# Later places on VectorE for the second half's delta rule, its convolution and pooling, and the last eight modulation sums

## The chip, the cores and the metric

The kernel runs on one core of a Trainium2 chip. The metric is the device time of one execution in microseconds; the figure for the kernel before is the median of three runs. One further execution was recorded by the hardware profiler, and all rows below come from it. Engines are named as in the profile: PE is TensorE (matmul) and PEld its weight loads, DVE is VectorE, ACT is ScalarE, POOL is GpSimd, and SP is SyncE, which issues most of the DMAs (SPq is its queue).

## What is computed

One layer of a streaming encoder for two groups of frames that share weights: a prompt of 1024 frames and a sample of 64 frames, width 1024. Cut to what matters:

```
mod = silu(c) @ w_ada + b_ada            # 6 x 1024: shift1, scale1, gate1, shift2, scale2, gate2
h   = rms_norm(x, norm_mix) * (1 + scale1) + shift1
u   = h @ w_in                           # columns of four mixers
mix = concat[conformer_conv, gated_deltanet, multiscale_pool, stick_breaking]
x   = x + gate1 * (mix @ w_out)
h2  = rms_norm(x, norm_ffn) * (1 + scale2) + shift2
x   = x + gate2 * ((silu(h2 @ w_gate) * (h2 @ w_up)) @ w_down)     # inner width 2816
```

The convolution mixer has 31 taps per channel and a layer norm; the delta rule works in chunks of 64 frames with a triangular solve in each and a state that goes from chunk to chunk; pooling takes windows of 2 to 16 frames; stick-breaking attention goes back over blocks of 128 keys. Besides `x`, the new caches and states are returned.

## The kernel before, in words

Everything is feature-major: a tile holds 128 features by up to 576 frames. The frames are cut in two halves: `HA` is prompt frames 0 to 511, `HB` is prompt frames 512 to 1023 with the 64 sample frames behind them. All products are in float32 made from three matmuls of rounded parts (`hi*hi`, `lo*hi`, `hi*lo`). So each weight tile of 128 x 1024 is loaded by SP (`load_w`, L320), rounded by ACT into `whi` and its rest taken by DVE into `wlo` (L330); activations are split in the same way into `hi` and `lo`. There are two buffers each for raw, `whi` and `wlo`.

The body (L1173 to L1188) calls the stages in this order: `in_proj(HA)`, `norm1(HB)`, `mixers(HA)`, `in_proj(HB)`, a part of the modulation sums, `out_proj(HA)`, the last eight modulation sums, `mixers(HB)`, `ffn(HA)`, `out_proj(HB)`, `ffn(HB)`. This is the order of tracing, not of execution: a planner replays the program against a time model and gives each engine one fixed queue. An instruction that is ready goes first by priority; priority follows the order of tracing, and what stands inside `tc.high_priority()` goes ahead of the rest. On the chip each engine then runs its queue in order and waits at the head of it.

The stages that the change touches:

- `out_proj` (L1035) loads the eight mixed tiles back from DRAM (`mixt`), splits them, makes 8 output tiles of 24 matmuls (`pg`), adds each to `x` (`residual`, L1029, tile `xA` or `xs`), sums squares into `acc`, and at the end runs the second norm (`modulate`, L308): a matmul over partitions (`pn`), Ln and Exp on ACT, and for each of eight tiles `nrm` (DVE), `hi` (ACT) and `lo` (DVE) in `modulate_k` (L297). For `HB` the splits of the mixed tiles go to `mixs`, on borrowed buffers, among them the buffer `raw` of the sample's modulation sums and of the delta rule.
- `ada_step` (L245) makes one modulation sum for the prompt: a load of 512 KB (`wadt`, in one of the two buffers `g0` and `g1`, which the feed-forward uses for its split too) and one DVE reduction. 24 of the 32 are made before `out_proj(HA)`; the last eight, for `gate2`, are traced behind it at high priority. `ada_sample` (L253) makes the 32 sums for the sample (`wads`, one buffer `raw`) inside `ffn(HA)` from the ninth tile on.
- `delta` (L855) runs short convolutions of four taps (`dnf`, `dn_feats`), decays, and `dn_group`: small batched matmuls, a triangular solve that goes out by DRAM (`nld`), is done on POOL (`fsn`, `fst`) and comes back by DRAM (`xd`, `X`), then the chain over chunks, and a store into `mixB`. For `HB` there are two groups of four chunks and one for the sample.
- `conv` (L870) makes for two tiles 31 taps each on DVE (`cy`, 606 columns for `HB`), a layer norm over partitions and a SiLU. `pool` (L984) makes ten sums on DVE and a small matmul.
- `ffn` (L1061) goes over 22 tiles in 11 chunks of two: gate and up products, the split `g` (`tg`, L1088 to L1091), and `down` for the chunk. In `ffn(HA)`, `conv(HB)` is traced at chunk 1 and `pool(HB)` at chunk 3. From chunk 6 on the products rotate over all eight PSUM banks. The last `down` of `HA` is held back and traced at the start of `ffn(HB)`.

`tc.issue_after(ins)`, which the kernel uses already for the modulation loads (`behind`, L317), puts every instruction that the block traces on the engine of `ins` behind `ins` in that engine's queue. Instructions of the block on other engines get no such place.

Of the kernel before, what the change touches and what calls it, by code (L numbers as in the profile page):

```python
# [11 lines left out]
ALU = mybir.AluOpType  # L12
# [16 lines left out]
KT = 8  # L29
FT = 22  # L30
FCH = 2
SAMP_DN = 515
SAMP_CV = 542
SAMP_PL = 527
# [25 lines left out]
def hybrid_encoder_kernel(ctx: ExitStack, tc: tile.TileContext, io):  # L60
    nc = tc.nc
# [5 lines left out]
    HA, HB = Half(), Half()  # L67
# [25 lines left out]
    def ST(name):  # L93
        return st.tile([P, 576], F32, tag="st", name=name)
# [18 lines left out]
    def act_(out, in_, func, bias=0.0, scale=1.0):  # L113
        nc.scalar.activation(out, in_, func, bias=bias, scale=scale)  # L114
# [5 lines left out]
        nc.vector.tensor_copy(out=out, in_=in_)  # L120

    def tt(out, a, b, op):
        nc.vector.tensor_tensor(out=out, in0=a, in1=b, op=op)  # L123

    def stt(out, a, s, b, op0, op1):
        nc.vector.scalar_tensor_tensor(out, a, s, b, op0, op1)  # L126

    def ts(out, a, s1, s2, op0, op1=None):
        if op1 is None:
# [13 lines left out]
    def f(ap):  # L143
        return ap.bitcast(F32)
# [152 lines left out]
    def modulate_k(h, k, r, sc, shift0, in_place):  # L297
        t = h.xt[k] if in_place else ST("nrm")
        h.hi.append(act.tile([P, 576], F32R, tag=f"hi{k}", name=f"hi{k}"))
        h.lo.append(act.tile([P, 576], F32R, tag=f"lo{k}", name=f"lo{k}"))  # L300
        for s0, w, g in h.segs:
            c = slice(s0, s0 + w)
            sh = mod[:, shift0 + k, g:g + 1]
            stt(t[:, c], h.xt[k][:, c], sc[:, k, g:g + 1], r[:, c], ALU.mult, ALU.mult)
            act_(h.hi[k][:, c], t[:, c], ACTF.Identity, bias=sh)
            stt(h.lo[k][:, c], t[:, c], sh, f(h.hi[k][:, c]), ALU.add, ALU.subtract)

    def modulate(h, acc, sc, shift0, in_place=False):  # L308
        r = rstd_of(h, acc, in_place)
# [3 lines left out]


    w_last = [None]

    def behind():  # L317
        return tc.issue_after(w_last[0])
# [551 lines left out]
    def conv(h):  # L870
        wn = SAMP_CV + 64 if h.samp else 512
        ys = []
        for i in range(2):
            g, e, buf = TT("cvg"), TT("cve"), TT("cvb")
            u = ud["cv", h.name]
            nc.sync.dma_start(out=g[:, 0:h.n], in_=u[2 * i + 1])
            nc.sync.dma_start(out=buf[:, 30:542], in_=u[2 * i, :, 0:512])
            if h.samp:
                copy_v(buf[:, 0:30], cvcar[:, i])
                nc.sync.dma_start(out=buf[:, 542:572], in_=io["ccs"][:, i])  # L880
                nc.sync.dma_start(out=buf[:, 572:636], in_=u[2 * i, :, 512:576])
            else:
                nc.vector.memset(buf[:, 0:30], 0.0)
            sigmoid_chain(e[:, 0:h.n], g[:, 0:h.n])
            tt(buf[:, 30:542], buf[:, 30:542], e[:, 0:512], ALU.mult)
            if h.samp:
                tt(buf[:, 572:636], buf[:, 572:636], e[:, 512:576], ALU.mult)
                nc.sync.dma_start(out=io["cv_s"][:, i], in_=buf[:, 606:636])
                nc.sync.dma_start(out=io["cv_p"][:, i], in_=buf[:, 512:542])
            else:  # L890
                copy_v(cvcar[:, i], buf[:, 512:542])
            y = fp.tile([P, 636], F32, tag=f"cy{i}", name=f"cy{i}")
            ts(y[:, 0:wn], buf[:, 0:wn], V("cw", 31 * i), V("cb", i), ALU.mult, ALU.add)
            for j in range(1, 31):
                stt(y[:, 0:wn], buf[:, j:j + wn], V("cw", 31 * i + j), y[:, 0:wn], ALU.mult, ALU.add)
            ys.append(y)
        hn = (wn + 1) // 2
        for c0 in range(0, wn, hn):
            n = min(hn, wn - c0)
            pm = PC("pmu")  # L900
            for i in range(2):
                mm(pm[:, 0:n], C("ones"), ys[i][:, c0:c0 + n], i == 0, i == 1)
            for i in range(2):
                stt(ys[i][:, c0:c0 + n], pm[:, 0:n], -1.0 / 256, ys[i][:, c0:c0 + n], ALU.mult, ALU.add)
        r = TT("cvr")
        sq = []
        for i in range(2):
            s = TT("cvs")
            act_(s[:, 0:wn], ys[i][:, 0:wn], ACTF.Square)
            sq.append(s)  # L910
        for c0 in range(0, wn, hn):
            n = min(hn, wn - c0)
            pm = PC("pvar")
            for i in range(2):
                mm(pm[:, 0:n], C("ones"), sq[i][:, c0:c0 + n], i == 0, i == 1)
            act_(r[:, c0:c0 + n], pm[:, 0:n], ACTF.Ln, bias=epst, scale=1.0 / 256)
        act_(r[:, 0:wn], r[:, 0:wn], ACTF.Exp, scale=-0.5)
        for i in range(2):
            y = ys[i]
            e = TT("cvz")  # L920
            tt(y[:, 0:wn], y[:, 0:wn], r[:, 0:wn], ALU.mult)
            ts(y[:, 0:wn], y[:, 0:wn], V("lng", i), V("lnb", i), ALU.mult, ALU.add)
            sigmoid_chain(e[:, 0:wn], y[:, 0:wn])
            tt(e[:, 0:wn], y[:, 0:wn], e[:, 0:wn], ALU.mult)
            nc.sync.dma_start(out=mixd[h.name][i, :, 0:512], in_=e[:, 0:512])
            if h.samp:
                nc.sync.dma_start(out=mixd[h.name][i, :, 512:576], in_=e[:, 542:606])
# [133 lines left out]
    def ffn(h):  # L1061
        if h.samp and DEFER:
            HA.last_down()
        n_ = h.n

        def gate(t):
            silu = h.samp or t >= SILU_T
            a = ST("fa")
            for ps, c0, n in gemm_fm(h, io["wgate"][t], h.hi, h.lo, KALL):
                with tc.high_priority():  # L1070
                    if not silu:
                        copy_a(a[:, c0:c0 + n], ps[:, 0:n])
                    else:
                        act_(a[:, c0:c0 + n], ps[:, 0:n], ACTF.Silu)
            if not silu:
                with tc.high_priority():
                    e = ST("fe")
                    sigmoid_chain(e[:, 0:n_], a[:, 0:n_])
                    tt(a[:, 0:n_], a[:, 0:n_], e[:, 0:n_], ALU.mult)
            return a  # L1080

        def up(t, a):
            j = t % FCH
            for ps, c0, n in gemm_fm(h, io["wup"][t], h.hi, h.lo, KALL):
                with tc.high_priority():
                    tt(a[:, c0:c0 + n], a[:, c0:c0 + n], ps[:, 0:n], ALU.mult)
            with tc.high_priority():
                tg = gp.tile([P, 1152], F32R, tag=f"g{j}", name=f"g{j}")  # L1088
                th, tl = tg[:, 0:576], tg[:, 576:1152]
                copy_a(th[:, 0:n_], a[:, 0:n_])  # L1090
                tt(tl[:, 0:n_], a[:, 0:n_], f(th[:, 0:n_]), ALU.subtract)  # L1091
            return th, tl

        def down(c, g, ms=range(KT)):
            mw = 8 // FCH
            for m in ms:
                if m % mw == 0:
                    w = load_w(io["wdown"][c, m // mw], 1024)
                o = (m % mw) * FCH * 128
                for ps, c0, n in gemm_fm(h, None, [t[0] for t in g], [t[1] for t in g], list(range(FCH)), w, o):  # L1100
                    with tc.high_priority():
                        residual(h, m, 40, ps, c0, n)
                if c == FT // FCH - 1:
                    nc.sync.dma_start(out=h.y[:, m], in_=h.xt[m][:, 0:n_])

        t0_s = 8
        a = gate(0)
        for c in range(FT // FCH):
            if not h.samp and c == 1:
                conv(HB)  # L1110
            if not h.samp and c == 3:
                pool(HB)
            g = []
            wide[0] = h.samp or c >= WIDE
            for j in range(FCH):
                if h.name == "A" and t0_s <= c * FCH + j:
                    s = c * FCH + j - t0_s
                    ada_sample(32 * s // (FT - t0_s), 32 * (s + 1) // (FT - t0_s))
                g.append(up(c * FCH + j, a))
                t = c * FCH + j + 1  # L1120
                a = gate(t) if t < FT else None
            if c == FT // FCH - 1 and DEFER and not h.samp:
                split_m = KT - 4 * DEFER
                down(c, g, range(split_m))
                h.last_down = lambda: down(c, g, range(split_m, KT))
            else:
                down(c, g)
# [34 lines left out]
        gemm_out(h, "pl", 2, 12)  # L1162

    def mixers(h):
        delta(h)
        sb_attn(h)
        if h.samp:
            sb_sample()
        else:
            conv(h)  # L1170
            pool(h)
# [7 lines left out]
        ada_step()  # L1179
    scale2(0)  # L1180
    out_proj(HA)
    with tc.high_priority():
        while ada_left:
            ada_step()
    mixers(HB)
# [179 lines left out]
```

## Time and profile before

| | us |
|---|---|
| median of three runs (lowest, highest) | 1485.28 (1483.03, 1486.69) |
| the profiled execution | 1488.28 |
| its span | 1486.4 |
| mean granted clock of TensorE | 0.975 |
| PE busy | 1405.1 (95%) |
| DVE busy | 1028.0 (69%) |
| ACT busy | 661.5 (45%) |
| POOL busy | 125.4 (8%) |

Busy is the time in which an engine has an instruction at work; matmul ends are modelled, so a busy TensorE is not one at its peak. The granted clock is a share of 2.4 GHz; it has two levels, 1.00 and 0.50 (1.2 GHz), and a value between them is a mean over a stretch. Times in rows are counted from the start of the span. In a row of a timeline the columns are start, duration, engine, line of the kernel, operation, output<-inputs and shapes, the number of merged instructions, and in brackets how long the engine stood before it and what ended that. A line is often that of a helper (L126 is every `scalar_tensor_tensor`, L138 every plain matmul); the tile's name tells which step it is.

### The profile page before, as it was taken

What the parts mean: (1) busy time and instruction counts of PE and PEld (TensorE: products, weight loads), DVE (VectorE), ACT (ScalarE), POOL (GpSimd) and SP (SyncE); (2) the same over time, 40 slices, a digit from 0 to 9 for tenths busy, and PEclk for the clock granted to TensorE, in tenths of its full rate; (3) what the DMA queues carried; (4) which work ended last, traced back from release to release, by engine and by line L of the source; (5) the groups of instructions that cost most, each with busy time, mean ns of one, the idle gap of its engine ahead of it and who ended that gap; (6) DMA issues with size and microseconds to landing.
All of it is one profiled execution on the core that took longest, in us unless ns stands there. A gap on an engine that the chain in (4) does not pass through costs nothing.

```text
span 1486.4 us, 24762 instructions
## 1 busy us (share of the span) xinstructions
PE 1405.1 (95%) x9824; PEld 1223.4 (82%) x9824; DVE 1028.0 (69%) x1816; ACT 661.5 (45%) x1191; POOL 125.4 (8%) x246
## 2 busy tenths in 40 slices
PE   8999999979987699799999899999899999999998
PEld 5777888858965477587777688889799999999998
DVE  7888897964799899766867666664744555544444
ACT  4457644745564368656755422222522222222221
POOL 0003100410004000600230000000000000000000
PEclk9999999989998899899999999999999999999999
DMA  8675655574745323424544454542322222222222
GB/s 294 239 228 166 202 168 166 155 213 146 260 153 168 75 75 95 123 81 129 161 113 153 155 186 154 177 158 83 110 92 86 86 82 77 84 86 86 86 83 95
DMA packets 98547, 205.43 MB, mean 138 GB/s; under 512 B 30848, under 2 KB 40928, under 8 KB 98432
## 3 DMA queue, kind: packets, MB, share of 16 engines
q1 hardware_dynamic: 89888, 191.68, 39.7%
q0 software_dynamic: 8544, 12.17, 3.9%
q8 instruction: 77, 1.26, 0.4%
q14 instruction: 38, 0.31, 0.1%
HBM read 175.57 MB, written 28.24 MB: 137 GB/s over the span
## 4 chain that ended last, share of the span: by engine, by line
PE 63%; DVE 17%; DMA 11%; issue 4%; ACT 3%; POOL 2%; SPq 1%; DVEq 0%; ACTq 0%; POOLq 0%
PE pg L138 57%; DMA wadt<-in_wadat_dram 4%; DVE cy L126 3%; DVE wlo L123 3%; DVE lo L126 1%; PE psC L141 1%; DMA X<-xd 1%; DVE dnf L126 1%; DVE junk L212 1%; PE pw L138 1%; PE z L141 1%; DVE wadt L212 1%; DVE nrm L126 1%; DMA raw<-udnB 1%; POOL fst L135 1%
## 5 line engine op out<-in xcount | busy, mean ns | idle before, releaser
L138 PE MATMUL pg<-hi,whi 128*128 128x288 f32 (+1 forms) x1504 | 504.8, 337 | 13.4 <-ACT whi L117 3.7
L138 PE MATMUL pg<-hi,wlo 128*128 128x288 f32 (+1 forms) x1504 | 499.7, 333 | 1.6 <-DVE wlo L123 1.6
L138 PE MATMUL pg<-lo,whi 128*128 128x288 f32 (+1 forms) x1504 | 498.7, 332 | 2.0 <-DVE lo L126 2.0
L117 ACT ACTIVATE whi<-wraw 128x1024 fp32r<-128x1024 f32 (+2 forms) x192 | 199.7, 1041 | 489.1 <-PE pg L138 419.4
L138 PEld LDWEIGHTS pg<-hi,whi 128*128 128x128 f32 x1504 | 285.4, 190 | 45.2 <-issue 5.7
L123 DVE TENSOR_TENSOR wlo<-wraw,whi 128x1024 fp32r<-128x1024 f32 (+2 forms) x192 | 230.6, 1202 | 111.9 <-ACT whi L117 107.4
L138 PEld LDWEIGHTS pg<-lo,whi 128*128 128x128 f32 x1504 | 285.6, 190 | 27.2 <-DVE lo L126 3.0
L138 PEld LDWEIGHTS pg<-hi,wlo 128*128 128x128 f32 x1504 | 285.0, 190 | 27.3 <-DVE wlo L123 3.2
L138 PE MATMUL pg<-g,whi 128*128 128x288 f32 (+1 forms) x1056 | 253.5, 331 | 3.0 <-DVE xA L126 1.9
L138 PEld LDWEIGHTS pg<-g,whi 128*128 128x128 f32 x1056 | 178.2, 189 | 20.1 <-DVE xA L126 4.3
L138 PE MATMUL pg<-g,wlo 128*128 128x288 f32 (+1 forms) x528 | 172.0, 329 | 0.0
L126 DVE SCALAR_TENSOR_TENSOR xs<-pg,mod,xs 128x288 f32<-128x288 f32 (+2 forms) x288 | 106.5, 412 | 85.7 <-PE pg L138 84.0
L138 PEld LDWEIGHTS pg<-g,wlo 128*128 128x128 f32 x528 | 99.6, 189 | 7.5
L123 DVE TENSOR_TENSOR fa<-fa,pg 128x288 f32<-128x288 f32 (+1 forms) x66 | 35.0, 531 | 101.8 <-PE pg L138 98.7
L126 DVE SCALAR_TENSOR_TENSOR cy<-cvb,vec,cy 128x512 f32<-128x512 f32 (+1 forms) x120 | 94.0, 796 | 0.2
L126 DVE SCALAR_TENSOR_TENSOR xA<-pg,mod,xA 128x512 f32<-128x512 f32 x96 | 69.3, 745 | 17.0 <-PE pg L138 16.4
L212 DVE CUSTOM_DVE_ANT_0 wadt<-wadt,cb,vec 128x1024 f32<-128x1024 f32 x32 | 41.0, 1282 | 22.8 <-DMA wadt<-in_wadat_dram 22.6
L114 ACT ACTIVATE e<-e 128x512 f32<-128x512 f32 (+4 forms) x100 | 52.1, 521 | 0.9
L138 PE MATMUL pg<-mixs,whi 128*128 128x288 f32 x256 | 50.8, 295 | 0.0
L212 DVE CUSTOM_DVE_ANT_0 wads<-wads,cb,vec 128x1024 f32<-128x1024 f32 x32 | 41.1, 1283 | 11.6 <-DMA wads<-in_wadat_dram 11.2
L114 ACT ACTIVATE zs<-zs 128x512 f32<-128x512 f32 (+4 forms) x50 | 25.9, 517 | 38.5 <-DVE zs L123 36.5
L138 PEld LDWEIGHTS pg<-mixs,whi 128*128 128x128 f32 x256 | 41.0, 188 | 0.1
(299 smaller groups left out, 1857.0 us busy)
## 6 DMA issues: line engine op xcount, KB each, us to landing
wraw<-in_wgate_dram SPq DMA_DIRECT2D x44, 512.0 KB, 3.3
wraw<-in_wup_dram SPq DMA_DIRECT2D x44, 512.0 KB, 3.2
wraw<-in_wdown_dram SPq DMA_DIRECT2D x44, 512.0 KB, 3.3
wadt<-in_wadat_dram SPq DMA_DIRECT2D x32, 512.0 KB, 4.7
wads<-in_wadat_dram SPq DMA_DIRECT2D x32, 512.0 KB, 4.1
wraw<-in_wfm_dram SPq DMA_DIRECT2D x30, 512.0 KB, 3.6
wraw<-in_wout_dram SPq DMA_DIRECT2D x16, 512.0 KB, 3.4
xA<-in_xa_dram SPq DMA_DIRECT2D x16, 256.0 KB, 5.2
```

The lines of the kernel that those rows point to most:

```text
L114: nc.scalar.activation(out, in_, func, bias=bias, scale=scale)
L117: nc.scalar.activation(out, in_, ACTF.Copy)
L123: nc.vector.tensor_tensor(out=out, in0=a, in1=b, op=op)
L126: nc.vector.scalar_tensor_tensor(out, a, s, b, op0, op1)
L135: nc.gpsimd.tensor_tensor(out=out, in0=a, in1=b, op=op)
L138: return nc.tensor.matmul(out, lhsT=lhsT, rhs=rhs, start=start, stop=stop)
L141: nc.tensor.matmul(out, lhsT=lhsT, rhs=rhs, start=start, stop=stop, skip_group_check=True)
L212: nc.vector.tensor_tensor_reduce(out=junk, in0=w, in1=cbt[g], scale=1.0, scalar=V("b_ada", col), op0=ALU.mult, op1=ALU.add, accum_out=mod[ ...
```

## The change

Three blocks get a place on DVE by `issue_after`. `tt` and `stt` now return their instruction, and `v_last` holds the last such instruction of two sites: the `lo` of a norm's tile (`modulate_k`) and the rest `tl` of a feed-forward tile (`up`).

- The last eight modulation sums are put behind the last `lo` of the first half's second norm.
- `delta(HB)` is put behind the same instruction; `delta(HA)` is not changed.
- `conv(HB)` and `pool(HB)` are traced together at chunk 5 of `ffn(HA)` instead of chunks 1 and 3, behind the `tl` of tile 9, the last of the fifth chunk.

```diff
+CONV_C = 5
...
     def tt(out, a, b, op):
-        nc.vector.tensor_tensor(out=out, in0=a, in1=b, op=op)
+        return nc.vector.tensor_tensor(out=out, in0=a, in1=b, op=op)
...
     def stt(out, a, s, b, op0, op1):
-        nc.vector.scalar_tensor_tensor(out, a, s, b, op0, op1)
+        return nc.vector.scalar_tensor_tensor(out, a, s, b, op0, op1)
...
-            stt(h.lo[k][:, c], t[:, c], sh, f(h.hi[k][:, c]), ALU.add, ALU.subtract)
+            v_last[0] = stt(h.lo[k][:, c], t[:, c], sh, f(h.hi[k][:, c]), ALU.add, ALU.subtract).ins
...
     w_last = [None]
+    v_last = [None]
...
-                tt(tl[:, 0:n_], a[:, 0:n_], f(th[:, 0:n_]), ALU.subtract)
+                v_last[0] = tt(tl[:, 0:n_], a[:, 0:n_], f(th[:, 0:n_]), ALU.subtract).ins
...
         for c in range(FT // FCH):
-            if not h.samp and c == 1:
-                conv(HB)
-            if not h.samp and c == 3:
-                pool(HB)
+            if not h.samp and c == CONV_C:
+                with tc.issue_after(v_last[0]):
+                    conv(HB)
+                    pool(HB)
...
     def mixers(h):
-        delta(h)
+        if h.samp:
+            with tc.issue_after(v_last[0]):
+                delta(h)
+        else:
+            delta(h)
         sb_attn(h)
...
     out_proj(HA)
-    with tc.high_priority():
+    with tc.high_priority(), tc.issue_after(v_last[0]):
         while ada_left:
             ada_step()
     mixers(HB)
```

## Rows read from the trace of the kernel before

**Rows 1.** The page, first part: busy us, share, instructions of each engine.
```profile
PE 1405.1 (95%) x9824; PEld 1223.4 (82%) x9824; DVE 1028.0 (69%) x1816; ACT 661.5 (45%) x1191; POOL 125.4 (8%) x246
```

**Rows 2.** Stretches: busy us (instructions) of each engine, granted clock, DMA share, GB/s.
```profile
407.00:410.00 3.00, 0.72 (x5) 0.41 (x3) 2.14 (x5) 1.15 (x3) 0.00 (x0) 1.00 0.56 201
410.00:527.00 117.00, 91.82 (x682) 68.45 (x683) 109.47 (x173) 59.46 (x106) 22.80 (x44) 0.88 0.44 125
527.00:620.00 93.00, 88.33 (x595) 68.09 (x593) 91.54 (x164) 74.33 (x148) 26.46 (x44) 0.98 0.37 111
...
775.00:984.00 209.00, 205.12 (x960) 164.23 (x959) 140.43 (x202) 74.39 (x112) 0.75 (x1) 0.99 0.51 166
840.00:976.00 136.00, 135.48 (x582) 110.54 (x582) 86.64 (x116) 40.83 (x51) 0.00 (x0) 0.99 0.54 175
1050.00:1075.00 25.00, 20.61 (x118) 17.87 (x116) 18.59 (x39) 14.40 (x26) 0.00 (x0) 0.93 0.26 86
```

**Rows 3.** DVE groups, 410 to 527 us: count | busy, mean ns | idle before.
```profile
L126 DVE SCALAR_TENSOR_TENSOR cy<-cvb,vec,cy 128x606 f32<-128x606 f32 x36 | 30.4, 851 | 0.0
...
L212 DVE CUSTOM_DVE_ANT_0 wadt<-wadt,cb,vec 128x1024 f32<-128x1024 f32 x8 | 10.1, 1276 | 4.5 <-DMA wadt<-in_wadat_dram 4.5
L126 DVE SCALAR_TENSOR_TENSOR dnf<-raw,vec,dnf 128x256 f32<-128x256 f32 x18 | 8.3, 486 | 0.0
...
L126 DVE SCALAR_TENSOR_TENSOR nrm<-xA,s,acc 128x512 f32<-128x512 f32 x8 | 5.6, 747 | 0.0
```

**Rows 4.** DVE timeline around the first half's second norm.
```profile
493.35 0.68 DVE L123 TENSOR_TENSOR acc<-acc,sq 128x512 f32<-128x512 f32 x1
...
500.45 1.28 DVE L212 CUSTOM_DVE_ANT_0 wadt<-wadt,cb,vec 128x1024 f32<-128x1024 f32 x1 [4.45 <-DMA wadt<-in_wadat_dram]
...
506.35 2.74 DVE L126 SCALAR_TENSOR_TENSOR nrm<-xA,s,acc 128x512 f32<-128x512 f32 x4
...
525.42 0.74 DVE L126 SCALAR_TENSOR_TENSOR lo<-nrm,mod,hi 128x512 fp32r<-128x512 f32 x1
```

**Rows 5.** ACT timeline there: the reciprocal root of the norm.
```profile
495.98 0.63 ACT L114 ACTIVATE acc<-acc 128x512 f32<-128x512 f32 x1
```

**Rows 6.** PE timeline at full clock: matmuls of 512 columns one after another.
```profile
414.85 0.39 PE L138 MATMUL pg<-hi,wlo 128*128 128x512 f32 x1
415.08 0.40 PE L138 MATMUL pg<-hi,whi 128*128 128x512 f32 x1
```

**Rows 7.** PE waits near 475, 620 and 760 us: us in total, times, longest.
```profile
PE pw L138 <- DMA X<-xd: 7.9, 1, 7.9
...
PE pw L138 <- DMA X<-xd: 6.3, 1, 6.3
...
PE pw L138 <- DMA X<-xd: 2.6, 1, 2.6
```

**Rows 8.** SP timeline: last stores of convolution, pooling and delta rule.
```profile
611.73 0.43 SPq L927 DMA_DIRECT2D mixB<-cvz  x1
...
684.38 0.43 SPq L1019 DMA_DIRECT2D mixB<-plm  x1
...
806.80 0.38 SPq L853 DMA_DIRECT2D mixB<-kbe  x1
```

**Rows 9.** DMA issues: count, KB each, us to landing.
```profile
wadt<-in_wadat_dram SPq DMA_DIRECT2D x32, 512.0 KB, 4.7
```

**Rows 10.** Instructions on the tile cy alone, 394 to 615 us: busy us, columns PE PEld DVE ACT.
```profile
394.00:615.00 221.00, 2.52 (x8) 1.44 (x8) 59.09 (x74) 2.61 (x4) 0.94 0.44 127
```

**Rows 11.** DVE timeline: first tap, a pooling sum, fifth chunk's last split, last sample sum.
```profile
396.31 0.59 DVE L132 TENSOR_SCALAR cy<-cvb,vec 128x606 f32<-128x606 f32 x1
...
602.15 0.78 DVE L123 TENSOR_TENSOR pls<-plb 128x605 f32<-128x605 f32 x1
...
775.14 0.68 DVE L123 TENSOR_TENSOR g<-fa,g 128x512 fp32r<-128x512 f32 x1
...
982.66 1.28 DVE L212 CUSTOM_DVE_ANT_0 wads<-wads,cb,vec 128x1024 f32<-128x1024 f32 x1 [0.44 <-DMA wads<-in_wadat_dram]
```

## The prediction

> **What bounds the kernel now.** The page's first part comes first: TensorE is busy 95% of the span, 1405.1 of 1486.4 us, and VectorE 69% [rows 1]. So a change that moves VectorE work can only win TensorE's waits and the time it runs at its lower clock. The stretches come next: they say where these are. In 840 to 976 us TensorE waits 0.5 us of 136 at clock 0.99, but from 410 to 527 us it is busy 91.8 of 117 us at a granted clock of 0.88, while VectorE is busy 109.5 of 117 [rows 2]. In that stretch stand the first half's output projection and its second norm. Third, the groups of VectorE there: 36 convolution taps of the second half take 30.4 us, the eight modulation sums 10.1 us, the delta rule's short convolution 8.3 us [rows 3]. None of these is what the norm waits for, yet they stand in its queue. The timeline shows it: the last partial sum of squares starts at 493.35 us, ScalarE has the reciprocal root at 496.6 (495.98 + 0.63), but the first `nrm` starts only at 506.35, because VectorE stood 4.45 us at a modulation sum whose weights had not landed, and then did another [rows 4, 5]. The last `lo` ends at 526.2.
>
> **What moves.** Three groups get a later place on VectorE. None gets a new semaphore: an instruction is only put behind another of the same engine; its followers on ScalarE, TensorE, GpSimd and SyncE's queue wait for its data as before.
>
> A. *Second norm freed.* Of the 109.5 us of VectorE in 410 to 527 the taps (30.4), the sums (10.1) and the delta rule (8.3 for its taps, and some twenty operations on 512 columns at the 0.68 us of such a row [rows 4]) leave, about 60 us in all. About 50 us stay. TensorE then sets the pace: one matmul of 512 columns starts each 0.227 us [rows 6], eight output tiles of 24 make 43.7 us, five attention blocks of eight such matmuls 9 us. The tail is a sum over partitions (1 us), Ln and Exp (1.3 us) and 16 operations of VectorE, four of which take 2.74 us together [rows 4], so 11 us. Thus 410 + 43.7 + 9 + 13 = 476 us for the last `lo`, 50 us earlier. But the 50 us are not the gain: the delta rule's matmuls that filled this stretch must still be done, so only TensorE's losses count. They are 3 - 0.72 = 2.3 us before 410, 25.2 us of waits after it, and the low clock: 0.88 over 117 us is 28 us at 1.2 GHz; part of it lies on the waits, 14 us I take as busy, half of it lost: 7. Together 34 us. New losses: without the delta rule the norm has little to cover it. The nearest row is the second half's own norm, 1050 to 1075 us, where the first half's held-back last down product (48 matmuls, 11 us) is the cover: 4.4 us of waits and clock 0.93 [rows 2], which is 6 us; without cover 6 + 11 = 17. Attention covers a little: I take 14. A = -34 + 14 = -20 us (bounds -28 and -17 by the two prices of the norm, and 0 if TensorE finds as little to do as before).
>
> The Trainium skill (Perfetto Trace Analysis, Optimization Strategy under Identifying Performance Opportunities) speaks against A: where the most-contended engine changes over time, it advises to interleave the regimes, and this change takes an interleaving apart. By that rule A would be about 0 and the sum +11 instead of -9. The rows so far go against it: the interleaved stretch 410 to 527 has the lowest clock and the most waits of those shown [rows 2]. It is a rival below.
>
> B. *Delta rule later.* Its three triangular solves go over GpSimd and DRAM, and each time TensorE, in order, stood at the result: 7.9, 6.3 and 2.6 us [rows 7]. The first lies inside A's losses; moved into the feed-forward it does not vanish, because feed-forward matmuls queued behind it stand as well. The nearest row is the second, which is already there: 6.3, and about 1 for the clock: B = +7 us (0 if the plan has enough ahead of it, +10 if it is the first one's 7.9 with its clock). SyncE's stores of the solve's input move along; a weight load queued behind one may come late: 0 to +3, I take 0, since two weight tiles are in flight. The delta rule's last store is at 806.8 us now [rows 8]. It starts at most some 90 us later than now, so it ends by 897; its output is needed near 984 us, so 87 us cover it, and what lies beyond would be paid in full.
>
> *Eight sums.* They cost 10.1 us behind the norm, beside the first feed-forward tiles. Two buffers and 4.7 us per load [rows 9] make three more rounds of 4.7 + 2 x 1.3, so they end near 476 + 22 = 498 us. Their buffers are those of the feed-forward's first split (needed by the first down product, some 27 us of matmuls after 476) and their values scale that product: covered by 5 us; uncovered at most 10.
>
> C. *Chunks 0 to 4 without the convolution.* In 527 to 620 VectorE is busy 91.5 of 93 us and TensorE loses 4.7 us of waits and 2 by the clock [rows 2]. The delta rule takes the convolution's place there, so little goes: -2 us (0 to -6).
>
> D. *Chunks 5 to 10 with convolution and pooling.* The convolution's operations are busy 59.1 us in 394 to 615 [rows 10], about 5 us more for its gates; neighbours overlap by 0.08 us (0.747 alone [rows 3], 2.74 for four), which leaves 57. Pooling has ten operations of about 0.78 us [rows 11]: 8. The fifth chunk's last split now starts at 775.1 us [rows 11]; from there to 984, where the last sample sum ends and the second half's projection gets its buffer, VectorE is busy 140.4 of 209 us [rows 2]. Add 65, and 10 for the delayed end of the delta rule: 215 us. VectorE reached 94% (109.5 of 117) and 98% (91.5 of 93) with such a mix; at 97% this takes 222 us. TensorE needs 209 and 7 for what comes with it, 216. D = 222 - 216 = +6 us (0 at full density, +12 at 94%). This is the term I trust least.
>
> **Sum.** -20 + 7 - 2 + 6 = -9 us. The profiled execution took 1488.28 us, 1.9 more than its span; that makes 1479.3. The median of the runs shown is 3.0 us lower, so 1476 for what is timed.
>
> **Rivals.**
>
> 1. *VectorE sets chunks 5 to 10 and takes the gain back.* If the fifth chunk ends only 12 us earlier and VectorE keeps 94% there, D is +12, and with B at +10 the sum is -20 + 10 - 2 + 12 = 0: 1485. For it: the 215 us against some 209. Against: conv taps are always ready, and filled VectorE to 98% in 527 to 620.
>
> 2. *The convolution comes late for the second half's projection: slower.* Now convolution and pooling go from 396.3 us (first tap) to 684.8 (last store), 288 us, the convolution alone to 612, 216 us [rows 8, 11]. From 760 us (775 less the 15 gained by A, B and C) they have until 975, 9 us before the projection's split less store and load. So it decides from 215 us on. At the convolution's own 216 us with 8 for store, load and split the end comes 9 us late: 1485; at the pace of both, 288, it is 73 late: 1549. The modulation sums for the sample columns stand in this queue too: the last starts at 982.66, just ahead of the split that needs its buffer [rows 11]; a delay there stops the projection as well. Against: the old pace was shared with a norm and the delta rule, the new one is not. As a typical price I take +20 over the forecast: 1496.
>
> 3. *More is won.* The first solve's stall finds cover (B = 0), the norm costs only 6 us (A = -28), and attention and delta rule, in a less crowded queue, save 6 us (C = -6), D = +6: -28: 1457.
>
> 4. *Un-interleaving costs what it saves* (A = 0): 7 - 2 + 6 = +11: 1496. For it: TensorE's other matmuls in 410 to 527 are gone. Against: 25 us of waits with them there.
>
> That the change does nothing is hardly possible: the taps stand in the norm's queue by name.
>
> **Chances.** Forecast 0.44 (its own range 1466 to 1481), rival 1 0.19 (1481 to 1490), rival 2 0.14, rival 3 0.16, rival 4 0.07. About 0.3%, 4.5 us, is what a measurement of this kernel can tell from no change. Faster: 0.42 of the forecast, all of rival 3 and a little of rival 1, 0.60. Slower: rivals 2 and 4 and a little of rival 1, 0.21. Within: 0.19. The range goes from 1455, which leaves half of rival 3's lower side out, to 1497, which leaves out rival 2's tail: 1455 to 1497.
>
> **What would show it.** A: no `cy`, `dnf` or `wadt` between the first `lo<-mixt` and the last `lo<-nrm`; that last `lo` near 476 us (before 490: right; after 505: wrong); waits and low clock there under 20 us. B: `pw` waiting for `X` three times, 15 us or more, now all in the feed-forward. Sums: no wait of `g` for `wadt`. C: TensorE waits in the first five chunks about as now. D: VectorE over 94% from the first convolution tap to the first split of `mixs`; the last `mixB<-cvz` before that split. The prediction is wrong if TensorE waits over 10 us ahead of the second half's projection for convolution, pooling or the sample sums, or if the last `lo` comes no earlier than 505 us.

## The result: 1.7% slower

The changed kernel takes 1509.64 us (median of four runs, 1508.08 to 1511.28), the kernel before on the same chip 1484.15: a ratio of 1.0173 [1.0149, 1.0198], 25 us slower. 1476 us were forecast, and 1455 to 1497 as the range. The profiled execution took 1509.31 us, its span 1507.4.

The first part of the page after, engine by engine, against [rows 1]: as many instructions on each engine, and TensorE busy 9.4 us longer, while the mean granted clock went from 0.975 to 0.962.

```profile
PE 1414.5 (94%) x9824; PEld 1227.7 (81%) x9824; DVE 1026.7 (68%) x1816; ACT 665.3 (44%) x1191; POOL 120.9 (8%) x246
```

Where the time went is read from stretches. First the changed kernel (columns as in [rows 2]: stretch, busy us and instructions of PE, PEld, DVE, ACT, POOL, granted clock, DMA share, GB/s):

```profile
250.00:380.00 130.00, 126.68 (x1219) 110.75 (x1218) 79.70 (x137) 71.36 (x149) 25.01 (x49) 0.99 0.65 205
410.00:527.00 117.00, 103.96 (x521) 79.95 (x520) 96.88 (x181) 75.04 (x138) 5.70 (x10) 0.93 0.41 119
527.00:620.00 93.00, 85.27 (x653) 68.06 (x652) 61.74 (x101) 57.73 (x108) 22.66 (x42) 0.94 0.34 88
711.00:1006.00 295.00, 258.80 (x1419) 200.18 (x1414) 225.02 (x347) 114.27 (x196) 23.23 (x46) 0.91 0.45 139
780.00:830.00 50.00, 38.11 (x206) 27.60 (x205) 49.59 (x86) 21.93 (x49) 9.15 (x14) 0.86 0.29 85
830.00:880.00 50.00, 32.14 (x179) 22.43 (x180) 25.66 (x48) 15.74 (x33) 10.83 (x28) 0.69 0.38 113
880.00:930.00 50.00, 46.73 (x201) 37.13 (x200) 32.47 (x43) 15.90 (x20) 0.00 (x0) 1.00 0.62 199
```

The kernel before, in the stretches of these that [rows 2] does not have:

```profile
250.00:380.00 130.00, 118.07 (x1122) 101.50 (x1121) 87.37 (x165) 75.89 (x166) 23.31 (x49) 0.93 0.55 168
...
780.00:830.00 50.00, 50.00 (x278) 38.73 (x278) 36.57 (x59) 27.55 (x50) 0.75 (x1) 1.00 0.48 156
830.00:880.00 50.00, 46.12 (x190) 36.37 (x189) 33.31 (x46) 17.75 (x25) 0.00 (x0) 0.97 0.53 169
880.00:930.00 50.00, 50.00 (x218) 40.84 (x218) 28.75 (x37) 13.25 (x16) 0.00 (x0) 1.00 0.49 163
```

I count as TensorE's loss in a stretch its idle time and the busy time times (1 - clock):

| stretch, us | before: idle + clock | after: idle + clock | after less before |
|---|---|---|---|
| 250 to 380 | 11.9 + 8.3 | 3.3 + 1.3 | -15.6 |
| 410 to 527 | 25.2 + 11.0 | 13.0 + 7.3 | -15.9 |
| 527 to 620 | 4.7 + 1.8 | 7.7 + 5.1 | +6.3 |
| 780 to 930 | 3.9 + 1.4 | 33.0 + 15.3 | +43.0 |

The sum is +17.8, and the span grew by 21.0 us. So 31.5 us are won in two stretches ahead of 527, and 43 are lost in 150 us. The stretches left out come to about +7 by the same measure, so it is some 4 us too high for the whole; it lies ahead of 250 us, where the profiles of all the kernels here differ by up to 11 us, that of e7 from the kernel before by 8. Chunks are counted from 0, as in the code: the fifth chunk is chunk 4, and `CONV_C = 5` is the one behind it. The next fence is VectorE's timeline after: the second norm's first `nrm`, its last `lo`, the fifth chunk's last split, the first tap and the last sample sum (against [rows 4, 11]).

```profile
449.53 0.74 DVE L127 SCALAR_TENSOR_TENSOR nrm<-xA,s,acc 128x512 f32<-128x512 f32 x1
...
461.21 1.41 DVE L127 SCALAR_TENSOR_TENSOR lo<-nrm,mod,hi 128x512 fp32r<-128x512 f32 x2
...
711.50 0.69 DVE L124 TENSOR_TENSOR g<-fa,g 128x512 fp32r<-128x512 f32 x1
...
717.21 0.60 DVE L133 TENSOR_SCALAR cy<-cvb,vec 128x606 f32<-128x606 f32 x1
...
1004.72 1.28 DVE L213 CUSTOM_DVE_ANT_0 wads<-wads,cb,vec 128x1024 f32<-128x1024 f32 x1 [1.49 <-DMA wads<-in_wadat_dram]
```

The norm is over at 462.6 us in place of 526.2, and the fifth chunk's split stands 63.6 us earlier. Much of that lead is mixers put off; what is left of it, and more, goes where they come due: the last sample sum, which frees the second half's projection, ends at 1006.0 us in place of 983.9. TensorE's waits after, 780 to 900 us (waiting matmul, what it waited for, us in total, times, longest):

```profile
PE pw L139 <- DMA X<-xd: 8.0, 1, 8.0
PE py L139 <- DVE W L124: 4.4, 2, 2.8
PE pg L139 <- DVE xA L127: 4.3, 1, 4.3
PE pg L139 <- DVE wlo L124: 4.0, 3, 1.6
PE psOs L142 <- ACT ph L118: 3.4, 1, 3.4
...
PE pvar L139 <- ACT cvs L115: 1.3, 1, 1.3
```

No wait is over 8.0 us. TensorE's timeline shows why they add up:

```profile
824.36 0.40 PE L139 MATMUL pg<-hi,wlo 128*128 128x512 f32 x1
...
831.19 0.42 PE L142 MATMUL psOs<-ph,v2s 128*128 128x64 f32 x1 [3.40 <-ACT ph L118]
...
834.29 2.37 PE L139 MATMUL pmu<-cy,cst 128*128 128x303 f32 x4
837.96 2.39 PE L139 MATMUL pvar<-cvs,cst 128*128 128x303 f32 x4 [1.31 <-ACT cvs L115]
848.32 0.45 PE L139 MATMUL pw<-cst,X 64*64 64x64 f32 x2 [7.97 <-DMA X<-xd]
...
854.39 0.69 PE L139 MATMUL py<-W,X 64*64 64x64 f32 x8 [1.63 <-DVE W L124]
854.87 0.64 PE L139 MATMUL px<-X,W 64*64 64x64 f32 x8
855.43 0.79 PE L139 MATMUL pg<-hi,whi 128*128 128x512 f32 x1
```

From 824.8 to 855.4 us its queue holds no feed-forward product (`pg`), only the sample attention (`psOs`, `psCs`), the convolution's layer norm (`pmu`, `pvar`) and the delta rule's sample group (`pw`, `py`, `px`), each waiting for the one before or for another engine. This is chunk 6, where the feed-forward begins to turn over all eight PSUM banks (`WIDE = 6`; `BANKS` is two of `mm`, two of `dn`, and `cv`, `z`, `c`, `o`). `dn` are the delta rule's, `cv` the convolution's, the last three the attention's. In the kernel before no mixer but the sample attention was left by then: convolution and delta rule had stored at 611.7 and 806.8 [rows 8].

Which bank the next product stood for can be read from the program. Each product takes the next entry of `BANKS`; the first of chunk 6, the up product of tile 12, is the program's 143rd and takes `o` (143 modulo 8 is 7), the bank of `psOs`. Gate and up product of tile 13, in `mm`, went ahead of it up to 824.8; the gate product of tile 14 has `dn`, and the downs need tile 12. The sample attention's last product ends near 834.5, but its four heads leave the bank one by one through a single buffer, `sbo`, and ScalarE twice waited until the head before was stored. The last of the four copies on VectorE ends at 854.6, and the product starts at 855.4:

```profile
845.01 0.22 ACT L118 ACTIVATE sbo<-psOs 64x64 f32<-64x64 f32 x1 [4.11 <-DMA mixB<-sbo]
...
854.36 0.22 DVE L124 TENSOR_TENSOR sbo<-psOs,sbo 64x64 f32<-64x64 f32 x1
```

### The profile page after: what moved, and what is told of

The parts are those of the page before. It is cut to its first block, busy times and chain, and to the rows that moved or that the text cites. A ratio compares the mean times of both kernels' runs of the same rounds, so it can differ in the third digit from the quotient of the medians.

```text
span 1507.4 us, 24783 instructions
## 1 busy us (share of the span) xinstructions
PE 1414.5 (94%) x9824; PEld 1227.7 (81%) x9824; DVE 1026.7 (68%) x1816; ACT 665.3 (44%) x1191; POOL 120.9 (8%) x246
## 4 chain that ended last, share of the span: by engine, by line
PE 69%; DVE 15%; DMA 7%; issue 3%; ACT 3%; POOL 1%; SPq 1%; DVEq 0%; ACTq 0%; POOLq 0%
PE pg L139 58%; DVE cy L127 2%; DVE wlo L124 2%; PE psC L142 2%; DMA wadt<-in_wadat_dram 2%; PE pk L139 2%; PE psO L142 1%; DVE xA L127 1%; ACT whi L118 1%; DMA wads<-in_wadat_dram 1%; DMA X<-xd 1%; PE z L142 1%; DMA mixt<-mixA 1%; DVE dnf L127 1%; DVE lo L127 1%
## 5 line engine op out<-in xcount | busy, mean ns | idle before, releaser
L115 ACT ACTIVATE fa<-pg 128x288 f32<-128x288 f32 (+1 forms) x52 | 22.3, 429 | 40.6 <-PE pg L139 40.5
```

## Experiments

Convolution here is always convolution with pooling. The expectations name three theories. **P**: from chunk 6 on the feed-forward needs banks that late mixers still hold, so its products can't be queued between them. **V**: VectorE, full of taps (49.59 of 50 us in 780 to 830), makes all behind it late. **Q**: the mixers' short chains cost the same wherever they stand. Each ratio is to the kernel before on the same chip.

| kernel | median us | ratio [95%] |
|---|---|---|
| e1 changed, two banks in all chunks | 1503.54 | 1.0164 [1.0137, 1.0191] |
| e2 changed, convolution behind chunk 1 | 1508.85 | 1.0197 [1.0165, 1.0229] |
| e3 convolution and pooling alone, chunk 5 | 1512.45 | 1.0225 [1.0195, 1.0255] |
| e4 delta rule and sums alone | 1497.51 | 1.0107 [1.0067, 1.0147] |
| e5 changed, WIDE 8 | 1496.91 | 1.0074 [1.0050, 1.0098] |
| e6 as e2, WIDE 8 | 1490.61 | 1.0052 [1.0033, 1.0071] |
| e7 before, WIDE 8 | 1492.35 | 1.0063 [1.0041, 1.0085] |
| e8 as e4, WIDE 8 | 1492.61 | 1.0064 [1.0040, 1.0087] |
| e9 convolution alone, chunk 1 | 1504.85 | 1.0140 [1.0097, 1.0183] |
| e10 convolution alone, chunk 3 | 1503.75 | 1.0137 [1.0091, 1.0184] |
| e11 as e3, WIDE 8 | 1491.96 | 1.0050 [1.0027, 1.0073] |
| e12 as e9, with the eight sums | 1510.26 | 1.0175 [1.0136, 1.0214] |
| f1 as e9, five banks in chunks 6 and 7 | 1488.63 | 1.0055 [1.0020, 1.0091] |
| f2 changed, same five banks | 1530.62 | 1.0338 [1.0295, 1.0381] |
| f3 before, same five banks | 1483.27 | 0.9997 [0.9978, 1.0015] |
| f4 as e9, WIDE 8 | 1494.90 | 1.0093 [1.0058, 1.0129] |
| g1 as f1, behind chunk 3 | 1477.36 | 0.9968 [0.9951, 0.9985] |
| g2 as f1, behind chunk 2 | 1473.34 | 0.9943 [0.9927, 0.9960] |

**The halves and the banks at all (e1 to e4).**

```
e1: -WIDE = 6      +WIDE = 11     # of 11 chunks: never
e2: -CONV_C = 5    +CONV_C = 1
e3: delta(h) and the eight sums without issue_after, as before
e4: conv(HB) at chunk 1 and pool(HB) at chunk 3 without issue_after, as before
```

> The changed kernel, with the first half's feed-forward kept to its own two PSUM banks in all eleven chunks (WIDE 11 in place of 6), so none of its products asks for a bank that the convolution's norm, the sample attention or the delta rule's sample group still holds. Theory P (banks): TensorE's loss between 780 and 905 us comes from products of chunks 6 and 7 that stand in order behind those banks; without them feed-forward products fill the gaps, and some 25 to 40 us return: 1470 to 1485 us. Theory V (VectorE is full, 99% in 730 to 830 us, and everything behind the convolution comes late): the banks are no cause, 1500 to 1512 us. Theory Q (the short products of the mixers stand in TensorE's queue one behind the other whatever the banks are): also 1500 to 1512.

> The changed kernel with convolution and pooling queued behind the first chunk's last split (CONV_C 1 in place of 5); the delta rule and the eight sums stay behind the second norm. Theory P: convolution and its norm are done near 700 us, ahead of chunk 6, and only the delta rule's sample group still holds a bank: 1475 to 1490 us, with the second norm still done near 462 us. Theory V: the crowding only moves into chunks 1 to 5, where taps and delta rule share VectorE: 1490 to 1505. If the delta rule's later place is the cause by itself: 1500 or more.

> The kernel before with only the convolution and pooling moved behind the fifth chunk; delta rule and eight sums where they were. Theory P: the convolution's norm and the sample attention come later than chunk 6's first product, which takes their banks: 1495 to 1515 us although nothing of the delta rule is late. If the delta rule's place is the cause: 1475 to 1490, since the second norm loses 30 us of taps ahead of it and nothing else is late.

> The changed kernel with convolution and pooling where they were before (chunks 1 and 3, no order edge); only the delta rule and the eight sums are behind the second norm. If the convolution's place is the cause of the loss: 1470 to 1485 us, with some of the gain at the norm gone since taps stand in its queue again. If the delta rule's place is the cause: 1495 or more, with TensorE's gaps at chunk 6 as in the changed kernel.

Each half alone is slower (e3, e4), so no one part is to blame, and the parts don't add: 33 and 16 us by the ratios against 25 together. An early convolution (e2) does not help: it came out above P's and V's numbers, where the delta rule's place by itself had been put. e1, which P put at 1470 to 1485, came out near the changed kernel. Its stretches show two things in one number:

```profile
830.00:880.00 50.00, 42.66 (x221) 32.11 (x220) 30.46 (x52) 24.52 (x36) 11.94 (x25) 0.91 0.38 116
...
930.00:980.00 50.00, 45.29 (x183) 34.54 (x182) 31.25 (x43) 11.65 (x14) 0.00 (x0) 0.97 0.50 176
```

The gap shrinks (busy 42.7 in place of 32.1, clock 0.91 in place of 0.69), but two banks lose 4.7 us in 930 to 980, where eight lose none. By idle and clock as above e1 loses 30 us in 780 to 930 where the changed kernel loses 48, and 22 in 930 to 1100 in place of 7. So the turn is worth having, only later. In e3 a product waits for a bank by name; here and below the columns are those of the waits, and this is 780 to 930 us of e3:

```profile
PE ppl L139 <- DVE plo L127: 7.7, 1, 7.7
PE pg L139 <- DVE xA L127: 7.3, 6, 2.7
PE pg L139 <- DVE sbo L124: 6.4, 1, 6.4
```

`sbo` is the copy that frees the sample attention's bank; a feed-forward product can wait for it only by that bank.

**The turn two chunks later (e5 to e8).** One line in each of four kernels:

```
-WIDE = 6
+WIDE = 8
```

> The changed kernel with the feed-forward's turn over all eight PSUM banks begun at chunk 8 (WIDE 8), when the mixers are done, in place of chunk 6. In the run with two banks throughout TensorE's gap at 830 to 880 us went from 17.9 to 7.3 us, but it then lost 4.7 us of 50 and more in 930 to 980, where chunks on eight banks lose nothing. Theory P (the turn over eight banks meets mixers that still hold theirs): both are had, 20 us less than 1503: 1480 to 1492 us. Theory V (VectorE full of taps in 730 to 830 is what makes the rest late): 1497 to 1510. Theory Q (the delta rule's solves and other short chains cost the same wherever feed-forward stands behind them): 1497 to 1510.

> As the run before this one, with convolution and pooling behind the first chunk (CONV_C 1, WIDE 8). Theory P with V (both the banks and the crowded VectorE have to go): 1470 to 1485 us. Theory P alone: as with CONV_C 5, 1480 to 1492. Theory Q: 1497 or more.

> The kernel before with WIDE 8 in place of 6, a control. Theory P: there the mixers are done when chunk 6 begins (last sample product at 825 us), so eight banks cost nothing in chunks 6 and 7 and two banks lose: 1490 to 1505 us, slower than before. If WIDE 8 is simply better, whatever the mixers do: below 1480, and the banks say nothing of the change.

> Delta rule and eight sums behind the second norm, convolution and pooling where they were, WIDE 8. Theory P: the 8.5 us stand at the sample group's solve at 840 to 848 us gets feed-forward products of two banks in front of it: 1472 to 1487 us. Theory Q: 1495 to 1500, as with WIDE 6.

The same line gains 1.0% on the changed kernel and 1.4% on e2, and costs the kernel before 0.6%. With WIDE 8 the change stands at 1.0074 / 1.0063 = 1.0011 (about [0.998, 1.004] from the two intervals) of its own before: of 25 us next to nothing is left, though no gain either. That is what shows P, as an interaction. But it returned less than P alone had promised: e5's 1496.9 lies above P's 1492, at the lower edge of what V and Q gave, and e8's 1492.6 lies between P's 1487 and Q's 1495. e5, 780 to 930 us, its stretches and waits:

```profile
780.00:830.00 50.00, 42.84 (x249) 31.60 (x249) 49.60 (x85) 25.21 (x54) 4.38 (x7) 0.93 0.38 116
830.00:880.00 50.00, 41.38 (x201) 30.73 (x200) 33.66 (x55) 23.03 (x33) 18.15 (x35) 0.90 0.36 110
880.00:930.00 50.00, 41.69 (x209) 31.36 (x208) 32.30 (x48) 21.15 (x32) 0.00 (x0) 0.93 0.61 186
```

```profile
PE pg L139 <- DVE xA L127: 12.8, 5, 5.5
PE pw L139 <- DMA X<-xd: 7.0, 1, 7.0
```

24.1 us are still idle there. 12.8 are products that wait for a bank whose result VectorE has not yet added (`xA`), behind taps; with the taps at chunk 1 (e6) that wait is 2.1 us, and 9.6 us are idle in all, as in the kernel before with the same line (e7). That is V's part; in the times it is 6 us, with intervals that overlap. The rows of e6 and e7:

```profile
780.00:930.00 150.00, 140.38 (x797) 108.86 (x794) 95.75 (x158) 73.58 (x128) 23.89 (x46) 0.98 0.49 146
...
780.00:930.00 150.00, 140.13 (x653) 108.01 (x652) 95.52 (x137) 57.00 (x88) 0.75 (x1) 1.00 0.48 152
```

**Convolution alone, and early (e9 to e12).**

```
e9, e10: as e3, with CONV_C = 1, 3;  e11: as e3, with WIDE = 8;  e12: as e9, and
-    with tc.high_priority():
+    with tc.high_priority(), tc.issue_after(v_last[0]):    # the eight sums
```

> The kernel before with only convolution and pooling moved, and only behind the first chunk's last split (CONV_C 1): the taps leave the second norm's queue, the delta rule stays early, and all mixers should be done before chunk 6 begins its turn over eight banks. Theory P: the gain at the norm stays (in the conv-only run with CONV_C 5 the lost time to 680 us was some 35 us less than before) and nothing is paid at chunk 6: 1460 to 1476 us. Theory Q or V (each gain there is paid later by the same work, wherever it stands): 1480 to 1495.

> The same behind the third chunk (CONV_C 3). Theory P: the convolution's norm now ends around chunk 6's first products; between the run with CONV_C 1 and that with CONV_C 5 (1512), near 1480 to 1495 us. Theory V: no difference to CONV_C 1, since VectorE has the same taps to do beside as many chunks.

> Convolution and pooling alone behind the fifth chunk (1512 us with WIDE 6), with WIDE 8. Theory P: the banks cost the convolution's half what they cost the whole change (12.7 us came back there): 1494 to 1502 us; the rest is the taps crowding VectorE (xA waits of 10 us and more stay). Theory V alone: 1507 to 1515.

> As the first of these (CONV_C 1, WIDE 6, delta rule early), with the eight sums behind the second norm as in the change. They cost the norm 10.1 us of VectorE and a 4.45 us stand: 3 to 10 us less than without, if nothing is late behind them; the same within 4 us if TensorE's own work sets the norm by then.

e11 returns 1.7% by the ratios, a little more than P expected. e9 and e10 missed P's number by 29 and by 9 us: I had taken convolution and delta rule for the only late mixers. TensorE's timeline of e9 shows the third:

```profile
859.66 0.28 PE L142 MATMUL psOs<-pl,v2s 128*128 128x64 f32 x1
873.74 0.77 PE L139 MATMUL pg<-hi,whi 128*128 128x512 f32 x1 [13.80 <-DVE sbo L124]
```

One product of chunk 6 stands 13.8 us, with all of TensorE behind it, for the bank of the sample attention: the up product of tile 12 again. Nothing in e9 has moved the attention in the code, yet its last product ends at 859.9 us in place of 824.9 before, while the last split ahead of chunk 6 stands only 8 us earlier (813.0, 820.7). So here it is mostly the mixer that came later. Whether the eight sums (e12) add a cost is not settled, the intervals of e9 and e12 overlap; the gain of 3 to 10 us that was one of the two expectations is not there.

**Which banks (f1 to f4).** Chunks 6 and 7 turn over the first five banks, without the attention's:

```
-        pool, tag = BANKS[turn[0] % 8] if wide[0] else BANKS[0]
+        pool, tag = BANKS[turn[0] % wide[0]] if wide[0] else BANKS[0]
...
-            wide[0] = h.samp or c >= WIDE
+            wide[0] = 8 if h.samp or c >= WIDE + 2 else 5 * (c >= WIDE)
```

> Convolution and pooling alone behind the first chunk (1505 us), with chunks 6 and 7 turning over five PSUM banks, without the three that the sample attention uses; from chunk 8 on over all eight. In the run with eight banks from chunk 6 a feed-forward product stood 13.8 us for `sbo`, the sample attention's result, and TensorE ran at its low clock behind it. Theory P: that stand goes with its clock, 15 to 25 us: 1480 to 1490. Theory Q (the losses of the mixers are the same wherever they stand, the bank wait is only where they show): 1498 or more.

> The changed kernel with the same five banks in chunks 6 and 7. There the convolution's norm and the delta rule's sample group, which hold the other three kinds of bank, run in chunk 6 too, so theory P expects less: 1498 to 1506 us, between 1509 (eight banks) and 1497 (two banks in these chunks). If the sample attention's banks alone were the cause: 1490 to 1497.

> The kernel before with the same five banks in chunks 6 and 7, a control: sample attention is over at 825 us there, ahead of chunk 6's second half. Theory P: 1482 to 1490, no gain. A gain of 8 us or more as in the changed kernel would say that the banks are a cost of every order and not of the change.

> Convolution and pooling alone behind the first chunk with WIDE 8. Theory P: as the other orders with WIDE 8 (1490.6 to 1496.9), 1485 to 1495 us, against 1505 with WIDE 6. Theory Q: 1500 or more.

This tells by which mixer is late. In e9 it was the attention: without its banks most of the loss comes back (f1, 1.0055 against 1.0140), although the attention is as late there, its last `sbo` copied at 877.0 us. In f1 830 to 880 us looks as follows; the profiled execution is the fastest of f1's ten (1478.66 us) and that of e9 the slowest of its five, so the rows make the difference larger than the medians do:

```profile
830.00:880.00 50.00, 50.00 (x211) 39.71 (x211) 30.90 (x47) 22.68 (x37) 0.00 (x0) 0.94 0.47 150
```

In the changed kernel delta rule and convolution are late too, and the five are `mm` and just theirs: 1.6% more is lost (f2, 1.0338 against 1.0173; I had expected a small gain, since I counted banks left out and not what the products are left with):

```profile
780.00:830.00 50.00, 31.15 (x169) 22.23 (x170) 49.16 (x88) 18.86 (x47) 6.94 (x12) 0.74 0.30 84
830.00:880.00 50.00, 30.54 (x168) 20.01 (x168) 21.21 (x40) 15.52 (x31) 9.86 (x30) 0.62 0.31 77
```

VectorE's load in these two stretches is that of the changed kernel or less, so V can't make this difference. Of five entries the 143rd product takes `dn` (143 modulo 5 is 3), and between these two rows of f2 TensorE has no feed-forward product for 63 us, in which the delta rule's sample group and the convolution's norm run to their end:

```profile
802.95 0.40 PE L139 MATMUL pg<-g,wlo 128*128 128x512 f32 x1
...
866.25 0.79 PE L139 MATMUL pg<-hi,whi 128*128 128x512 f32 x1
```

In the kernel before, where convolution and delta rule are done, the same edit does nothing (f3). TensorE's idle time in 780 to 930 us, from one profile of each kernel, puts the runs side by side:

| order | eight banks from chunk 6 | eight from chunk 8 | five in 6 and 7 |
|---|---|---|---|
| before | 3.9 | 9.9 (e7) | 2.4 (f3) |
| changed, convolution behind chunk 5 | 33.0 | 24.1 (e5) | 48.4 (f2) |
| changed, behind chunk 1 | 25.8 (e2) | 9.6 (e6) | |
| convolution alone, chunk 5 | 37.2 (e3) | 21.4 (e11) | |
| convolution alone, chunk 1 | 22.9 (e9) | 12.1 (f4) | 2.6 (f1) |
| delta rule and sums alone | 19.2 (e4) | 10.3 (e8) | |

The later turn takes 9 to 16 us away in every changed order and adds 6 in the kernel before. In the changed kernel the banks are not all of it: the convolution's place is worth about 7 us with the early turn and 14 with the late one. f4 came out where P put it. Q, by which nothing would change, falls.

**Is the gain at the norm real (g1, g2)?** As f1, with `CONV_C = 3` and `CONV_C = 2`.

> Convolution and pooling alone behind the third chunk (1504 us), with five banks, without the sample attention's three, in chunks 6 and 7. There a product stood 11.7 us for `sbo`, and TensorE lost less ahead of 730 us than with CONV_C 1 (the convolution's products at 580 to 630 no longer meet the attention). Theory P: the 16 us that the same edit gave back with CONV_C 1, 1480 to 1490, and 1475 if the smaller loss ahead of 730 stays; below 1484 it would beat the kernel before. Theory Q: 1498 or more.

> The same behind the second chunk (CONV_C 2). Theory P: as with CONV_C 1 and 3, 1478 to 1490 us. Theory Q: 1498 or more.

Yes: g2 takes 1473.34 us, 0.57% less than the kernel before (0.9943 [0.9927, 0.9960]), less than P's 1478 to 1490, and, by the ratios, 2.3% less than the changed one. Since the banks alone bring nothing (f3), this is the convolution out of the norm's queue. It is the best of three places: f1, behind chunk 1, loses as little in 410 to 527 (16 us, g2 17, before 36) and is still slower than the kernel before, so the place where the taps go counts as well. g2's stretches:

```profile
410.00:527.00 117.00, 104.33 (x771) 80.88 (x767) 91.71 (x151) 69.33 (x127) 26.11 (x46) 0.96 0.47 143
...
780.00:830.00 50.00, 47.69 (x219) 37.23 (x217) 34.41 (x52) 26.86 (x47) 4.02 (x6) 1.00 0.63 173
830.00:880.00 50.00, 49.46 (x215) 39.15 (x215) 33.60 (x50) 23.87 (x38) 0.00 (x0) 0.97 0.47 153
```

## Why the prediction was wrong

- **A, second norm freed (-20): right, and earlier than said.** The last `lo` ends at 462.6 (476 forecast), with no `cy`, `dnf` or `wadt` of the moved groups ahead of it; 15.9 us were won there by the table. It is mostly the convolution's part: 410 to 527 loses 17 us in e9 and in g2, and 32 in e4. Not foreseen: 15.6 us in 250 to 380, where TensorE had stood 7.0 us for `X` and 3.0 for `W` of the first half's own delta rule, and after 0.7 and none. All kernels with a late delta rule lose 3 to 10 us there, all others 16 to 23; by which step was not traced. Rival 4 (A = 0) falls: this interleaving cost more than it covered. The Trainium skill (Perfetto Trace Analysis, Optimization Strategy) says that interleaving such regimes may improve performance; in 410 to 527 us it did not, with 36.2 us lost interleaved and 20.3 apart.
- **B, delta rule later (+7): a little low.** `pw` stood for `X` 7.7, 2.7 and 8.0 us, now all in the feed-forward. The waits in 527 to 720 and the 8.0 above:

```profile
PE pw L139 <- DMA X<-xd: 10.8, 3, 7.7
```

  Of before's, 8.9 us lay outside A's stretch [rows 7]; so +10 for waits, at the upper bound given. The last of the three, 8.0, stands in D's stretch and is counted there by the table.
- **Eight sums hidden:** the last of them starts at 490.3 us, ahead of the first `g` at 496.6, and no wait for `wadt` shows; e12 leaves a cost open.
- **C, chunks 0 to 4 (-2):** +6.3 in 527 to 620, mostly the first `X` with its clock, which B had counted.
- **D, chunks 5 to 10 (+6): the step that failed.** It asked how many microseconds VectorE and TensorE each have to do from the fifth chunk's last split to the projection, and took the larger, 222. The stretch took 294.5 (711.5 to 1006.0). VectorE's work was well sized, 225.0 us against 215, but it filled 76% of the stretch and not 97%: 99% in 780 to 830, with the taps, and half of 830 to 880. From the first tap to the first split of `mixs`, where over 94% was the sign, it was busy 85%:

```profile
717.20:875.60 158.40, 126.53 (x804) 92.76 (x802) 135.32 (x223) 74.16 (x145) 23.23 (x46) 0.84 0.36 104
```

  In 780 to 930 alone TensorE lost 43 us more than before. D priced no order of short products and no PSUM bank, and what it left out stands in the description of the kernel: chunk 6 begins to use the mixers' banks. The change makes the mixers later (the sample attention's last copy by 12 us, delta rule by 71, convolution by 256) and chunk 6 earlier, and both count in the same place. With the turn two chunks later the change costs 0.1% in place of 1.7% (e5 against e7); the taps that crowd VectorE in the same stretch are the other part (e5 against e6).
- **Signs and rivals.** Neither sign by which the prediction called itself wrong came true: the last `lo` was early, and no wait of 10 us for convolution, pooling or sample sums stands ahead of the projection. Rival 1 (VectorE) has a part: its `xA` waits are 4.3 us of 33.0 idle in the changed kernel, and 12.8 of 24.1 once the banks are out of the way (e5). 2 came nearest in its time, 1496 and at worst 1549 (its sum at 216 us counts store and load twice, in the 8 and in the 9: the end would be 1 us late, not 9), with the wrong place: the convolution's last store, in SyncE's timeline after, is far ahead of the projection, and it was late for chunk 6. The point from which a mixer is late was not the projection's 975 us but the first product in one of its banks.

```profile
867.25 0.47 SPq L929 DMA_DIRECT2D mixB<-cvz  x1
```

The Trainium skill (Perfetto Trace Analysis, Matmul Optimizations) asks that all eight PSUM banks be used. The control bears it out (two chunks fewer on eight banks cost the kernel before 0.6%), and the changed kernel bounds it: there the same two chunks on eight banks cost 1.0%, with mixers still in some of the other six; and five banks in these two chunks served the kernel before as well as eight (f3, 0.9997).

What stays open: no row names the reason for an order. That the changed kernel holds no `pg` from 824.8 to 855.4 us because of the banks is concluded from the program's turn, from the copy that ends 0.8 us ahead of the next product, and from e5, f1 and f2. How much the single buffer `sbo` costs was not tried. Why the sample attention ends near 860 us in e9 was not traced.

## What to carry to other kernels

Before work is moved on one engine's queue, list what it holds until it is done (accumulator banks, buffers) and find the place in the program from which something else takes these; if that place is counted in steps of another stage, making that stage faster moves it too. Price a crowded stretch by its longest chain and by who stands in order behind it, not only by the busier engine's sum; to find the chain, look for a stretch in which the main stage has no product in the queue, not only for a long wait. When a gain vanishes, cross the suspected neighbour's switch with and without the change: an interaction (here -1.0% and +0.6%) says more than either run.

## What the runs showed of the hardware

TensorE does not only stand in such a chain, it also runs slowly: in the changed kernel's 830 to 880 us it was busy 32 of 50 us at clock 0.69, in f2 30.5 at 0.62. The clock was worth about a third of the loss (15.3 of 48.3 us). And the times of one program spread, some more than others: f1's ten runs go from 1478.66 to 1500.56 us, those of the kernel before beside them from 1478.24 to 1490.20, the changed kernel's four within 3.2. With such a spread a few runs do not settle a difference of 10 us.
